# Three small moves in a hybrid encoder block: a wider product of channel factors, key reads on another queue, and additions on another engine

## The chip, the cores and the metric

The kernel runs on one core of a Trainium2 chip. A core has a matrix engine (PE), three engines for elementwise work (Vector, here DVE; Scalar, here ACT; GpSimd, here POOL) and a sync engine (SP), each with an instruction stream of its own that it works through in order, and 16 DMA engines that move data between the core's on-chip memory (SBUF) and the chip's main memory. Matrix products land in PSUM, eight banks of 512 float32 columns. DMAs are issued by SP, ACT or POOL, each with a queue. The metric is the time of the whole program on the device in microseconds.

## The reference

One layer of an encoder block, applied with the same weights to a batch of 512 tokens and one of 256 (768 rows in all), model width 2048, everything in float32:

```
h = rmsnorm(x, ln_mix_g); z = h @ w_in                 # 2048 -> 1024 fourier | 1024 q | 256 k | 256 v
of = einsum('bsgc,gcd->bsgd', Re(fft2(zf)), w_f)       # 8 groups of 128 channels, over (positions, channels)
q, k = apply_rope(q), apply_rope(k)
oa = window_attention(q, k, v, sink)                   # 16 q heads, 4 kv heads, +-128 positions
x = x + concat(rmsnorm(of), rmsnorm(oa)) @ w_out
h = rmsnorm(x, ln_mlp_g); u = relu(h @ w_up)
x = x + (u * u) @ w_down                               # 8192 wide
y = rmsnorm(x, ln_final_g)
```

## The kernel before, in words

Matrix products are done as three products of rounded halves: each operand is split into a high part (rounded for the fast matrix path, ACT) and a low remainder (DVE subtracts), and high x high, high x low and low x high are added up in PSUM. The helper `split` (L66) does both halves. Large products (the Fourier columns of `w_in`, `w_up`, `w_down`) are taken by a seven-product scheme on 2 x 2 blocks.

The program runs in stages: the values and the Fourier columns of `w_in` (to about 174 us), then twenty pieces of `w_in` for keys and queries (to 378 us), the attention together with the Fourier half of `w_out` (to 589 us), the attention half of `w_out` (to 731 us), then `w_up` and `w_down`. PE's order is that in which the code is written. On the other engines a scheduler orders the work in the pieces' stage; from the last piece on their order too is written out, by events with due times.

In the stage of pieces, PE works through the pieces (`pz`, L802, 48 matmuls each), and other work is hung on half pieces by `after(piece, fn)`:

- The Fourier groups. `load_group(g)` (L543) reads the group's map `wf` and its columns `zf` by SP. `fold(g)` (L559) forms the channel factors: the cosine and sine tables of the channels (`cc`) times the group's `w_fourier`, a product `pc` in plain float32 (L566), whose split is `cw`; it also folds the positions into sums and differences `s`. One piece later `stage1` multiplies these with `cw` (`pa`), and half a piece and a piece later the rest of `stage1` and `stage2` follow (`pe`, `pz2`). Group g's `fold` is hung on piece g + 0.5, so that of the next group comes right behind the first part of `stage1` of this one. `pc`, `pa`, `pe` and `pz2` share four PSUM banks.
- The rotation of keys and queries. `cross` (L682) multiplies by the sines on POOL (`zy`), `turned` and `parts` finish on DVE and ACT, and ACT's queue writes high and low parts of the keys (`kh`, `kl`) and the queries to main memory. `load_k(i)` (L717) reads the keys back, twice for each part, into the two halves of the partitions of `kdh` and `kdl`, four reads in all; they are hung on pieces 14.5 to 17.5.

In the attention, units of one block and one group of heads follow each other; PE forms the scores `s` (L848), DVE takes row maxima (L863), ACT the exponentials, POOL scales by the row sums (L893), PE transposes (L905) and multiplies by the values (L924). Finished row tiles of 128 tokens are read back by `load_oa` (L956): `parts_of` splits them for the product with `w_out`; `squares` squares both halves on ACT (L972) and adds them, and `reduce` (L975) sums over the head dimension on DVE into `sr`. There are six row tiles; for five the squares stand in `oar`, for the last in `cx`.

Of the kernel before, what the change touches and what calls it, by code (L numbers as in the profile page):

```python
# [11 lines left out]
F32 = mybir.dt.float32  # L12
F32R = mybir.dt.float32r
BF16 = mybir.dt.bfloat16
AF = mybir.ActivationFunctionType
ALU = mybir.AluOpType
# [4 lines left out]
P = 128  # L21
# [10 lines left out]
NKV = 4  # L32
# [8 lines left out]
def hybrid_encoder(ctx: ExitStack, tc: tile.TileContext, a: dict):  # L41
    nc = tc.nc
    ctx.enter_context(tc.manual_schedule(engines={mybir.EngineType.PE}))

    def f32(ap):
        return ap.bitcast(F32)
# [19 lines left out]
    def split(hi, lo, src, scale=None):  # L66

        if scale is None:
            nc.scalar.activation(hi, src, AF.Copy)
            nc.vector.tensor_tensor(out=lo, in0=src, in1=f32(hi), op=ALU.subtract)  # L70
        else:
            nc.scalar.activation(hi, src, AF.Copy, scale=scale)
            nc.vector.scalar_tensor_tensor(
                out=lo, in0=src, scalar=scale, in1=f32(hi), op0=ALU.mult, op1=ALU.subtract
            )
# [41 lines left out]
    kr_d = [dpool.tile([2 * P, T], F32, tag=f"k{c}", name=f"k{c}") for c in "hl"]  # L117
# [35 lines left out]
    raws = {}  # L153
# [44 lines left out]
    with ExitStack() as ph:  # L198
        hp = ph.enter_context(tc.tile_pool(name="hp", bufs=1, reuse_waits="tile"))
        pp = ph.enter_context(tc.tile_pool(name="pp1", bufs=4, space=PSUM))  # L200
# [338 lines left out]
        fp = fctx.enter_context(tc.tile_pool(name="fp", bufs=1, reuse_waits="tile"))  # L539
        cc = fp.tile([P, 2, P], F32, tag="cc", name="cc")  # L540
        ssf = fp.tile([P, T], F32, tag="ssf", name="ssf")
        fst = {}
        def load_group(g):  # L543
            wf = fp.tile([P, P], F32, tag="wf", name="wf", bufs=2)
            nc.sync.dma_start(wf[:], a["w_fourier"][g])
            z = fp.tile([P, T], F32, tag="zf", name="zf", bufs=2)
            nc.sync.dma_start(z[:], zf_d[g][:])
            fst[g] = (z, wf)

        nc.sync.dma_start(cc[:], a["c_chan"])  # L550
        load_group(0)
        tabh = fp.tile([P, 4, 256], F32R, tag="tabh", name="tabh")
        tabl = fp.tile([P, 4, 256], F32R, tag="tabl", name="tabl")
# [5 lines left out]
        def fold(g):  # L559

            z, wf = fst.pop(g)
            nc.vector.tensor_tensor(out=z[:], in0=z[:], in1=rb[:], op=ALU.mult)
            pc = pp.tile([P, 512], F32, tag="f", bufs=4, name="pc")
            cw = fp.tile([P, 2, 2, P], F32R, tag="cw", name="cw", bufs=2)
            for i in range(2):
                nc.tensor.matmul(pc[:, i * P : (i + 1) * P], cc[:, i, :], wf[:], start=True, stop=True)  # L566
            split(cw[:, 0], cw[:, 1], pc[:, :256].rearrange("p (s d) -> p s d", s=2))
            e = fp.tile([P, 320], F32, tag="fe", name="fe")
            o = fp.tile([P, 256], F32, tag="fo", name="fo")
            s = fp.tile([P, 6, P], F32, tag="fs", name="fs")  # L570
            tt = lambda out, x, y, op: nc.vector.tensor_tensor(out=out, in0=x, in1=y, op=op)
            add, sub = ALU.add, ALU.subtract
            tt(e[:, 1:256], z[:, 1:256], z[:, 511:256:-1], add)
            nc.scalar.copy(e[:, 0:257:256], z[:, 0:257:256])
            tt(o[:, 1:256], z[:, 1:256], z[:, 511:256:-1], sub)
            tt(s[:, 0, :], e[:, 0:128], e[:, 256:128:-1], add)
            tt(s[:, 1, :], e[:, 0:128], e[:, 256:128:-1], sub)
            nc.scalar.copy(s[:, 2, 0:1], e[:, 128:129])
            tt(s[:, 2, 1:128], o[:, 1:128], o[:, 255:128:-1], sub)
            tt(s[:, 3, 0:127], o[:, 1:128], o[:, 255:128:-1], add)  # L580
            nc.scalar.copy(s[:, 3, 127:128], o[:, 128:129])
            nc.scalar.copy(s[:, 4, 0:1], z[:, 512:513])
            tt(s[:, 4, 1:128], z[:, 513:640], z[:, 767:640:-1], add)
            nc.scalar.copy(s[:, 5, 0:1], z[:, 640:641])
            tt(s[:, 5, 1:128], z[:, 513:640], z[:, 767:640:-1], sub)
            sh = fp.tile([P, 6, P], F32R, tag="sh", name="sh")
            sl = fp.tile([P, 6, P], F32R, tag="sl", name="sl")
            split(sh[:], sl[:], s[:])
            ah = fp.tile([P, 6, P], F32R, tag="ah", name="ah")
            al = fp.tile([P, 6, P], F32R, tag="al", name="al")  # L590
            fst[g] = (sh, sl, cw, ah, al)
# [63 lines left out]
        kt = {}  # L655
# [60 lines left out]

        def load_k(i):  # L717
            h = slice(i % 2 * HD, (i % 2 + 1) * HD)
            nc.sync.dma_start(f32(kt["kdh" if i < 2 else "kdl"][h]), kr_d[i // 2][:].rearrange("(d h) t -> d h t", h=NKV))

        units = [(b, g) for b in range(NM) for g in range(NKV)]
        state = {}
# [14 lines left out]
        for g in range(FG):  # L737
            p0 = (0.5, 1.5, 2.5, 3.5, 4.5, 5.5, 6.5, 7.5)[g]
            if g > 0:
                after(p0 - 1, lambda g=g: load_group(g))  # L740
            after(p0, lambda g=g: fold(g))
            for b in range(3):
                after(p0 + 1 + (b == 2) * 0.5, lambda g=g, b=b: stage1(g, b))
            after(p0 + 2, lambda g=g: stage2(g))
# [10 lines left out]
        for i in range(4):  # L755
            after(14.5 + i, lambda i=i: load_k(i))
# [31 lines left out]
        for piece in range(n_in):  # L788
# [7 lines left out]
            for c in range(2):  # L796
                cs = slice(c * P, (c + 1) * P)
                for i in range(4):
                    first, stop = j == 0 and i == 0, j == 3 and i == 3
                    for w, o, n in ((wh, 0, 0), (wh, 1, 1), (wl, 0, 2)):  # L800
                        for s in range(2):
                            nc.tensor.matmul(  # L802
                                ps[c][s][:, :HALF], w[:, i, cs], whole[j // 2][s][o][:, 4 * (j % 2) + i, :],
                                start=first and n == 0, stop=stop and n == 2,
# [24 lines left out]
    op = out_ctx.enter_context(tc.tile_pool(name="op", bufs=1, reuse_waits="tile"))  # L829
# [3 lines left out]
    mask, sink, kdh, kdl = (kt[c] for c in ("mask", "sink", "kdh", "kdl"))  # L833
# [116 lines left out]
    def oa_tiles(m):  # L950

        oa[m] = [
            op.tile([P, 8, P], F32R, tag=f"of{c}{m - 1}", name=f"oa{c}{m}") for c in "hl"
        ] + [op.tile([P, P], F32, tag=f"sr{m}", name="sr")]

    def load_oa(m, when=lambda dt, fn: fn(), spare=None):  # L956

        oa_tiles(m)
        oh, ol, sr = oa[m]
        if spare is None:  # L960
            raws = [op.tile([P, 4, P], F32, tag="oar", name="oar", bufs=2)[:] for _ in range(2)]
        else:
            raws = spare
        for i, raw in enumerate(raws):
            nc.sync.dma_start(raw, oa_d[m][i * 512 : (i + 1) * 512, :].rearrange("(k p) t -> p k t", p=P))

        def parts_of(i):
            split(oh[:, 4 * i : 4 * i + 4, :], ol[:, 4 * i : 4 * i + 4, :], raws[i])

        def squares():  # L970
            for raw in raws:
                nc.scalar.activation(raw, raw, AF.Square)  # L972
            nc.gpsimd.tensor_tensor(out=raws[1], in0=raws[1], in1=raws[0], op=ALU.add)

        def reduce():  # L975
            nc.vector.tensor_reduce(out=sr[:], in_=raws[1].rearrange("p k t -> p t k"), op=ALU.add, axis=AX.X)

        when(t_oa0, lambda: parts_of(0))
        when(t_oa1, lambda: parts_of(1))
        when(max(t_sq, t_oa0, t_oa1), squares)  # L980
        when(max(t_red, t_sq, t_oa0, t_oa1), reduce)
# [22 lines left out]
    for u in range(len(units)):  # L1004
        t = pace * u + t_first
# [423 lines left out]
    pp = ctx.enter_context(tc.tile_pool(name="pp5", bufs=4, space=PSUM, reuse_waits="tile"))  # L1429
# [382 lines left out]
```

## Time and profile before

| | |
|---|---|
| median of 3 runs | 2591.28 us (2590.07 to 2592.25) |
| the profiled execution | 2589.57 us |
| its span, first to last instruction | 2587.7 us |
| granted PE clock | 0.999 of full speed |
| PE busy | 2576.2 us (100% of the span) |
| DVE, ACT, POOL busy | 1812.2, 1124.0, 257.8 us |
| moved by DMA | 489.55 MB |

A row of a group reads: line, engine, operation, output <- inputs, shapes, count, then busy us, mean ns of one, and idle us before it with what ended it. A row of a timeline or of the chain in order of time starts with its start and its duration in us; the brackets hold the idle time before it and what ended that. A row of a waiting list reads: us in total, times, the longest. A row of a windows table has the stretch, its length, the busy us of PE, PEld (weight loads), DVE, ACT and POOL with their instructions, the granted clock, the DMA engines' busy share and GB/s.

### The profile page before, as it was taken

To read this page: it belongs to the slowest core of one execution; us is meant where nothing else is said; L and a number is where in the kernel's file an instruction comes from. 1 tells how busy PE (TensorE), PEld (TensorE's weight loads), DVE (VectorE), ACT (ScalarE), POOL (GpSimd) and SP (SyncE) were. 2 spreads that over 40 slices of the span, in tenths; PEclk is the share of its full clock that TensorE was granted. 3 is DMA by queue.
4 is the path that set the end of the run, shared out by engine and by line. 5 is a ranking of instruction groups with operands and counts; after the bars stand their busy time and mean duration, and the time that the engine had idled before them with its cause. 6 is when DMAs were issued, how large, how long until landed. Compare 5 with 4: busy or idle time off the path is not lost.

```text
span 2587.7 us, 34958 instructions
## 1 busy us (share of the span) xinstructions
PE 2576.2 (100%) x13580; PEld 2358.4 (91%) x13580; DVE 1812.2 (70%) x2216; ACT 1124.0 (43%) x1574; POOL 257.8 (10%) x359
## 2 busy tenths in 40 slices
PE   9999999999999999999999999999999999999998
PEld 9999998888899999999999999988888888888887
DVE  7966568777555656555877877667776765777687
ACT  6545437674333333333444544433333333333335
POOL 1001332233201011000000000110000000000000
PEclk9999999999999999999999999999999999999999
DMA  7963385345664445456666666675543662555364
GB/s 252 311 226 113 127 240 181 117 135 193 223 193 157 163 160 186 161 190 238 213 214 232 229 215 208 248 301 178 182 156 111 220 232 82 179 179 164 96 209 155
DMA packets 268999, 489.55 MB, mean 189 GB/s; under 512 B 19568, under 2 KB 164000, under 8 KB 267424
## 3 DMA queue, kind: packets, MB, share of 16 engines
q1 hardware_dynamic: 197328, 321.26, 39.3%
q10 hardware_dynamic: 58688, 115.18, 11.7%
q0 software_dynamic: 12816, 50.87, 5.8%
q8 instruction: 107, 1.75, 0.3%
q14 instruction: 60, 0.49, 0.1%
HBM read 360.35 MB, written 126.88 MB: 188 GB/s over the span
## 4 chain that ended last, share of the span: by engine, by line
PE 98%; DVE 1%; DMA 1%; issue 0%; ACT 0%; DVEq 0%; SPq 0%; POOLq 0%; POOL 0%; ACTq 0%
PE pu L1193 36%; PE pd L1628 35%; PE pm L1046 9%; PE pz L802 6%; PE p L268 5%; PE pv L391 1%; PE o L924 1%; PE s L848 1%; PE t L905 1%; PE pe L630 0%; PE pa L609 0%; PE ptx L137 0%; DMA raw<-in_w_in 0%; PE pt L137 0%; DMA qs<-ql 0%; PE pz L630 0%
## 5 line engine op out<-in xcount | busy, mean ns | idle before, releaser
L1193 PE MATMUL pu<-xf,wh 128*128 128x384 f32 x3072 | 780.1, 334 | 0.0
L1193 PEld LDWEIGHTS pu<-xf,wh 128*128 128x128 f32 x3072 | 554.0, 188 | 1.5 <-ACT o L1211 1.1
L1628 PE MATMUL pd<-wl,sh 128*128 128x512 f32 x1332 | 517.8, 389 | 0.0
L1628 PE MATMUL pd<-wh,sh 128*128 128x512 f32 x1332 | 517.8, 389 | 0.0
L1628 PE MATMUL pd<-wh,sl 128*128 128x512 f32 x1332 | 517.6, 389 | 0.0
L1193 PE MATMUL pu<-xf,wl 128*128 128x384 f32 x1536 | 513.2, 334 | 0.0
L1605 ACT ACTIVATE wh<-rd 128x1024 fp32r<-128x1024 f32 x200 | 202.4, 1054 | 522.2 <-PE pd L1628 421.8
L1615 DVE TENSOR_TENSOR wl<-rd,wh 128x1024 fp32r<-128x1024 f32 x200 | 236.1, 1221 | 226.3 <-ACT wh L1605 225.5
L1173 ACT ACTIVATE wh<-ur 128x1024 fp32r<-128x1024 f32 x160 | 170.0, 1063 | 382.7 <-PE pu L1193 216.8
L1628 PEld LDWEIGHTS pd<-wh,sh 128*128 128x128 f32 x1332 | 250.0, 188 | 51.9
L1628 PEld LDWEIGHTS pd<-wl,sh 128*128 128x128 f32 x1332 | 250.0, 188 | 51.9
L1628 PEld LDWEIGHTS pd<-wh,sl 128*128 128x128 f32 x1332 | 249.9, 188 | 51.8 <-DVE sl L1616 0.3
L1193 PEld LDWEIGHTS pu<-xf,wl 128*128 128x128 f32 x1536 | 288.3, 188 | 0.0
L1179 DVE TENSOR_TENSOR wl<-ur,wh 128x1024 fp32r<-128x1024 f32 x160 | 195.4, 1221 | 75.4 <-ACT wh L1173 75.4
L1214 DVE TENSOR_TENSOR o<-pu,o 128x768 f32<-128x768 f32 x160 | 152.8, 955 | 123.3 <-PE pu L1193 115.1
L1598 DVE TENSOR_TENSOR rd<-rd 128x1024 f32<-128x1024 f32 x112 | 131.7, 1217 | 0.0
L1193 PE MATMUL pu<-xs,wh 128*128 128x384 f32 x512 | 129.8, 334 | 0.0
L1173 ACT ACTIVATE wh<-sx 128x1024 fp32r<-128x1024 f32 x64 | 67.9, 1062 | 130.4 <-PE pu L1193 101.9
L268 PE MATMUL p<-xs,wh 128*128 128x384 f32 x448 | 113.8, 334 | 0.0
L1616 DVE TENSOR_TENSOR sl<-sr,sh 128x768 fp32r<-128x768 f32 x111 | 105.5, 950 | 0.0
L1179 DVE TENSOR_TENSOR wl<-sx,wh 128x1024 fp32r<-128x1024 f32 x64 | 78.1, 1222 | 24.1 <-ACT wh L1173 23.9
L1193 PEld LDWEIGHTS pu<-xs,wh 128*128 128x128 f32 x512 | 92.4, 188 | 0.0
(279 smaller groups left out, 3921.9 us busy)
## 6 DMA issues: line engine op xcount, KB each, us to landing
rd<-in_w_down SPq DMA_DIRECT2D x176, 512.0 KB, 5.2
ur<-in_w_up SPq DMA_DIRECT2D x128, 512.0 KB, 3.9
sr<-sd SPq DMA_DIRECT2D x95, 384.0 KB, 5.4
pd<-o ACTq DMA_DIRECT2D x60, 384.0 KB, 2.3
o<-pd POOLq DMA_DIRECT2D x60, 384.0 KB, 6.0
sd<-sm ACTq DMA_DIRECT2D x60, 384.0 KB, 2.8
raw<-in_w_in SPq DMA_DIRECT2D x38, 512.0 KB, 6.0
raw<-in_w_out SPq DMA_DIRECT2D x32, 512.0 KB, 4.5
```

The lines of the kernel that those rows point to most:

```text
L268: nc.tensor.matmul(ps7[bank, g, r][:, :HALF], l[:, i, r * P : (r + 1) * P], x[:, o, 4 * e + i, :], start=(opens and e == 0 and i == 0 and ...
L802: nc.tensor.matmul(ps[c][s][:, :HALF], w[:, i, cs], whole[j // 2][s][o][:, 4 * (j % 2) + i, :], start=first and n == 0, stop=stop and n == 2,)
L1046: nc.tensor.matmul(ps, l(k), w[:, k % 2, :], start=(k == 0 and n == 0), stop=(k == 7 and n == 2))
L1173: nc.scalar.activation(wh[:], raw[:], AF.Copy)
L1179: nc.vector.tensor_tensor(out=wl[:], in0=raw[:], in1=f32(wh[:]), op=ALU.subtract)
L1193: nc.tensor.matmul(ps[:, t, :HALF], w[:, i, t * P : (t + 1) * P], xb[:, o, i, :], start=(s == first_of[bank] and i == 0 and n == 0), stop= ...
L1214: nc.vector.tensor_tensor(out=o, in0=src, in1=o, op=ALU.add)
L1598: add = lambda x, y, op: nc.vector.tensor_tensor(out=x[:], in0=x[:], in1=y[:], op=op)
L1605: nc.scalar.activation(wh[:], t[:], AF.Copy)
L1615: nc.vector.tensor_tensor(out=wl[:], in0=t[:], in1=f32(wh[:]), op=ALU.subtract)
L1616: nc.vector.tensor_tensor(out=sl[:], in0=sr[:], in1=f32(sh[:]), op=ALU.subtract)
L1628: nc.tensor.matmul(o, l[:, q, ts], w[:, ns], start=(j == j0 and (q, t) == (0, 0)), stop=(j == j1 and (q, t) == (1, 2)),)
```

## The change

Three edits. The channel factors of two Fourier groups are formed at once: the maps of groups g and g + 1 (g even) are read by one DMA and stand side by side, one product per table has 256 columns in place of 128, one split of 512 columns makes both groups' `cw`, and the odd group's `fold` takes its half from there. The four reads of the rotated keys are issued on GpSimd's queue in place of SP's. The sum of the two squared halves of an attention row tile is formed by Vector in place of GpSimd.

```diff
-        fst = {}
+        fst, cws = {}, {}
         def load_group(g):
-            wf = fp.tile([P, P], F32, tag="wf", name="wf", bufs=2)
-            nc.sync.dma_start(wf[:], a["w_fourier"][g])
+            if g % 2 == 0:
+                wf = fp.tile([P, 2, P], F32, tag="wf", name="wf")
+                nc.sync.dma_start(wf[:], a["w_fourier"][g : g + 2].rearrange("g c d -> c g d"))
+            else:
+                wf = None
...
             nc.vector.tensor_tensor(out=z[:], in0=z[:], in1=rb[:], op=ALU.mult)
-            pc = pp.tile([P, 512], F32, tag="f", bufs=4, name="pc")
-            cw = fp.tile([P, 2, 2, P], F32R, tag="cw", name="cw", bufs=2)
-            for i in range(2):
-                nc.tensor.matmul(pc[:, i * P : (i + 1) * P], cc[:, i, :], wf[:], start=True, stop=True)
-            split(cw[:, 0], cw[:, 1], pc[:, :256].rearrange("p (s d) -> p s d", s=2))
+            if wf is not None:
+                pc = pp.tile([P, 512], F32, tag="f", bufs=4, name="pc")
+                cws["now"] = fp.tile([P, 2, 2, 2, P], F32R, tag="cw", name="cw", bufs=2)
+                for i in range(2):
+                    nc.tensor.matmul(pc[:, i * 256 : (i + 1) * 256], cc[:, i, :], wf[:].rearrange("c g d -> c (g d)"), start=True, stop=True)
+                both = [cws["now"][:, o].rearrange("p g s d -> p (g s) d") for o in range(2)]
+                split(*[x.rearrange("p (g s) d -> p s g d", g=2) for x in both], pc[:].rearrange("p (s g d) -> p s g d", s=2, g=2))
+            cw = cws["now"][:, :, g % 2]
...
         def load_k(i):
             h = slice(i % 2 * HD, (i % 2 + 1) * HD)
-            nc.sync.dma_start(f32(kt["kdh" if i < 2 else "kdl"][h]), kr_d[i // 2][:].rearrange("(d h) t -> d h t", h=NKV))
+            nc.gpsimd.dma_start(f32(kt["kdh" if i < 2 else "kdl"][h]), kr_d[i // 2][:].rearrange("(d h) t -> d h t", h=NKV))
...
         def squares():
             for raw in raws:
                 nc.scalar.activation(raw, raw, AF.Square)
-            nc.gpsimd.tensor_tensor(out=raws[1], in0=raws[1], in1=raws[0], op=ALU.add)
+            nc.vector.tensor_tensor(out=raws[1], in0=raws[1], in1=raws[0], op=ALU.add)
```

Line numbers behind the edit are shifted by 3 to 6: L566 becomes L570, L719 becomes L725, L973 becomes L979.

## The prediction

> **What bounds the kernel now.** I read the page's first table and its chain of waits, then the list of waits on PE, then, place by place, the chain in order of time, the timelines and the windows around the three edits.
>
> ```profile
> span 2587.7 us, 34958 instructions
> PE 2576.2 (100%) x13580; PEld 2358.4 (91%) x13580; DVE 1812.2 (70%) x2216; ACT 1124.0 (43%) x1574; POOL 257.8 (10%) x359
> PE 98%; DVE 1%; DMA 1%; issue 0%; ACT 0%; DVEq 0%; SPq 0%; POOLq 0%; POOL 0%; ACTq 0%
> ...
> PE pv L391 <- ACT wh L69: 1.1, 1, 1.1
> PE pw L474 <- DVE mhalf L56: 1.0, 1, 1.0
> PE s L848 <- DMA qs<-ql: 0.4, 1, 0.4
> PE pt L137 <- DVE xr L452: 0.2, 1, 0.2
> PE pt L137 <- DMA xt<-in_x_prompt: 0.2, 1, 0.2
> ```
>
> The chain that ended last is PE for 98% of the span, and the whole list of what PE waited for adds up to 2.9 us, of which only the 0.4 us for `qs` lies after the first 60 us. So this is a PE program nearly from end to end: an edit shortens the run only by what it takes out of PE's own stream, and lengthens it only by making PE wait where it doesn't now. A microsecond won on DVE, POOL or SP is worth nothing by itself. The profiled execution took 2589.57 us, 1.87 us more than its span of 2587.7, and is 1.71 us under the median of 2591.28; I work out differences and apply them to the median.
>
> **The change, first edit: two groups' channel factors at once.** This one alone touches PE's stream. In the chain of waits in order of time, the product `pc` of a group shows as one piece, and the summary line of the stretch from 174 to 302 us gives its share:
>
> ```profile
> by line: PE pz L802 71.8%; PE pe L630 8.9%; PE pa L609 8.7%; PE pz L630 4.5%; PE pc L566 3.1%; PE pa L598 1.8%; PE pa L599 0.8%; PE ps_r L648 0.5%
> ...
> 186.44 0.44 PE pc L566 x4
> 222.01 0.50 PE pc L566 x4
> 231.56 1.43 PE pe L630 x12
> ```
>
> 3.1% of 128 us is 4.0 us for eight groups, 0.50 us each. A group has two matmuls in the program and four records (x4), so each matmul of plain float32 runs as two records, 0.125 us per record. In PE's order the second group of each pair loses its product:
>
> ```order
> L599 MATMUL pa<-cw,sl 128x128
> L609 MATMUL pa<-cw,sh 128x256 x2
> L609 MATMUL pa<-cw,sl 128x256
> L609 MATMUL pa<-cw,sh 128x128 x2
> L609 MATMUL pa<-cw,sl 128x128
> L566 MATMUL pc<-wf,cc 128x128 x2
> L802 MATMUL pz<-xs_291,wh 128x384
> ```
>
> That is the place before, in the second group; now:
>
> ```order
> L605 MATMUL pa<-cw,sl 128x128
> L615 MATMUL pa<-cw,sh 128x256 x2
> L615 MATMUL pa<-cw,sl 128x256
> L615 MATMUL pa<-cw,sh 128x128 x2
> L615 MATMUL pa<-cw,sl 128x128
> L808 MATMUL pz<-xs_291,wh 128x384
> ```
>
> The row of `pc` is gone, and the first group's row reads 128x256 x2 in place of 128x128 x2: half the records with twice the columns. No float32 product in the trace has more than 128 columns, so the price of a wide record is bounded. End A: it costs what a 256-column record of the rounded type costs, 1.43 / 12 = 0.119 us. Then a pair takes 4 x 0.119 = 0.48 us instead of 2 x 0.50 = 1.00, and four pairs save 4 x 0.52 = 2.1 us. End B: time goes with columns, a record takes 0.25 us, and nothing is saved. Two sets of rows from PE's timeline pull either way:
>
> ```profile
> 233.67 0.22 PE L599 MATMUL pa<-cw,sl 128*128 128x128 f32 x1
> 233.73 0.34 PE L598 MATMUL pa<-cw,sh 128*128 128x256 f32 x1
> ...
> 594.79 0.50 PE L1367 MATMUL pr<-ones,sr 128*128 128x1 f32 x4
> 595.15 0.49 PE L1046 MATMUL pm<-wh,oah 128*128 128x512 f32 x1
> ```
>
> A 128-column record of the rounded type is followed after 0.06 us, half of a `pc` record's step: plain float32 looks bound by columns, at half the rate (end B). But four float32 records of a single column also take 0.36 us, 0.09 each: there is a floor that has nothing to do with columns, and halving the records saves it (end A). The row of the same kind, `pc` itself, stands only a little above that floor. I take a third of the way from B to A, a gain of 0.7 us, and keep 0 to 2.1 for the range. A loss is excluded here: the columns are the same in all, and the records half.
>
> The Trainium skill (FP8 and Floating Point Precision, TensorE Precision Notes) says that true FP32 takes four passes through the array, two halves against two halves. The trace agrees as far as it goes, with two records of twice the usual step. By that rule the wide product costs its full columns and the term would be end B, zero.
>
> The split of `cw` becomes one 512-column operation in the first group and none in the second. Its price: the same split of a 512-column bank in the attention,
>
> ```profile
> L909 DVE TENSOR_TENSOR tl<-t,th 128x512 fp32r<-128x512 f32 x56 | 37.8, 677 | 2.5 <-ACT th L908 2.5
> ...
> 226.30 0.41 DVE L70 TENSOR_TENSOR cw<-pc,cw 128x256 fp32r<-128x256 f32 x1
> ...
> 232.27 0.28 DVE L70 TENSOR_TENSOR al<-pa,ah 1x128 fp32r<-1x128 f32 x1
> ...
> 233.43 0.28 PE L630 MATMUL pz<-tabh,al 128*128 128x256 f32 x1
> ```
>
> 0.68 against 0.41 us, so DVE's row in the first group of a pair runs 0.27 us later and in the second 0.41 earlier. Behind it the tightest consumer is the last `al` row, done at 232.55 and read by PE at 233.43: 0.88 us of cover, so I cost the delay at nothing. If ACT's longer half adds as much again (0.5 us in all) the cover still holds; were it gone entirely, four groups could lose at most 0.5 us each, 2 us. The four `wf` loads dropped from SP's queue were issued without PE waiting, and the one that is left per pair is needed as late as before: nothing.
>
> **Second edit: the key reads move to POOL's queue.** They leave SP, where each stood in line behind a weight load, and come to stand on POOL:
>
> ```order
> L687 TENSOR_TENSOR zy<-zs,sinr 128x256 x28
> L893 TENSOR_SCALAR p<-p,rs 128x256 x8
> L893 TENSOR_SCALAR p<-p,rs 128x384 x12
> L687 TENSOR_TENSOR zy<-zs,sinr 128x256 x2
> L893 TENSOR_SCALAR p<-p,rs 128x384 x8
> ```
>
> That is POOL around the rotation before (`zy` is the crossed product with the sines), and now:
>
> ```order
> L693 TENSOR_TENSOR zy<-zs,sinr 128x256 x12
> L725 DMA kdh<-kh 64x3072 x2
> L725 DMA kdl<-kl 64x3072 x2
> L693 TENSOR_TENSOR zy<-zs,sinr 128x256 x16
> L899 TENSOR_SCALAR p<-p,rs 128x256 x8
> ```
>
> All four stand after the twelfth `zy` and hold the other sixteen behind them. The timelines say whether that is a wait:
>
> ```profile
> 320.57 6.65 POOL L687 TENSOR_TENSOR zy<-zs,sinr 128x256 f32<-128x256 f32 x4 [1.99 <-DVE zs L696]
> 344.50 0.73 POOL L687 TENSOR_TENSOR zy<-zs,sinr 128x256 f32<-128x256 f32 x1 [17.27 <-ACT zs L815]
> ...
> 324.48 0.37 ACTq L704 DMA_DIRECT2D kl<-zs  x1
> ...
> DMA to landing us min/median/max: 2.1/2.5/4.6
> ...
> 339.67 0.51 SPq L719 DMA_DIRECT2D kdl<-kl  x1
> 344.04 0.47 SPq L719 DMA_DIRECT2D kdl<-kl  x1
> ...
> L848 PE MATMUL s<-kdl,qs x96: 274/281/421, 378.0 to 573.6; 128*128 128x256 f32 x64, 128*128 128x384 f32 x32
> ```
>
> The last write of the keys goes out at 324.48 and lands some 2.5, at most 4.6, us later (the row for those writes), by 329.1; POOL ends its twelfth `zy` at 327.2 and has nothing to do until 344.5. So the four reads go out some 12 us sooner than the last ones on SP, inside a hole of 17.27 us, and PE first reads the keys at 378.0. The other side is traffic:
>
> ```profile
> 323.00:345.00 22.00, 22.00 (x127) 21.64 (x126) 12.86 (x16) 7.82 (x8) 4.72 (x4) 1.00 0.94 278
> ...
> 333.12 0.40 SPq L79 DMA_DIRECT2D raw<-in_w_in  x1
> ...
> 337.22 2.01 DVE L70 TENSOR_TENSOR wl<-raw,wh 128x1024 fp32r<-128x1024 f32 x1 [2.57 <-ACT wh L69]
> 341.58 2.01 DVE L70 TENSOR_TENSOR wl<-raw,wh 128x1024 fp32r<-128x1024 f32 x1 [2.36 <-ACT wh L69]
> ...
> 302.85 75.20 PE pz L802 x431
> ```
>
> From 323 to 345 us the DMA engines are 94% busy, and the same 3.1 MB (four times 64 x 3072 floats) now come earlier in that stretch and compete with the weight load of 333.12. The pieces of `w_in` whose low halves are done at 339.2 and 343.6 are the last but two and the last but one. The last nine pieces run as one block on PE from 302.85 for 75.20 us, 8.36 each, so PE opens these two at 353.0 and 361.3: covers of 13.8 and 17.7 us. A load later by even 10 us costs nothing.
>
> **Third edit: DVE adds the squares.** Six additions of 512 columns leave POOL (1.29 us each) and come to DVE. In DVE's order at the third row tile, before:
>
> ```order
> L863 ISA p,mx<-s,mask,sink 128x256
> L863 ISA mx 128x1
> L868 TENSOR_SCALAR nm<-mx 128x1
> L976 TENSOR_REDUCE sr<-oar 128x128
> L863 ISA p,mx<-s,mask,sink 128x256
> ```
>
> and now, the same place (`oar` the squares, `p,mx` the row maxima that free a score bank):
>
> ```order
> L869 ISA p,mx<-s,mask,sink 128x256
> L869 ISA mx 128x1
> L874 TENSOR_SCALAR nm<-mx 128x1
> L979 TENSOR_TENSOR oar<-oar 128x512
> L982 TENSOR_REDUCE sr<-oar 128x128
> L869 ISA p,mx<-s,mask,sink 128x256
> ```
>
> The new row waits for ACT's squares, with row maxima, `tl` splits and the normalising factors queued behind it. DVE's waiting list and the timelines of that tile:
>
> ```profile
> DVE p L863 <- PE s L848: 7.7, 13, 0.9
> DVE sr L976 <- POOL oar L973: 2.7, 3, 1.6
> ...
> 565.50 1.14 ACT L972 ACTIVATE oar<-oar 128x512 f32<-128x512 f32 x2
> ...
> 566.31 0.15 DVE L868 TENSOR_SCALAR nm<-mx 128x1 f32<-128x1 f32 x1
> 568.11 1.09 DVE L976 TENSOR_REDUCE sr<-oar 128x128 f32<-128x512 f32 x1 [1.64 <-POOL oar L973]
> ...
> L70 DVE TENSOR_TENSOR oal<-oar,oah 128x512 fp32r<-128x512 f32 x10 | 7.4, 738 | 1.9 <-ACT oah L69 1.9
> ```
>
> ACT ends the squares at 566.64, 0.2 us after DVE gets there; the addition costs what the like-sized `oal` row costs, 0.74 us, and the reduction starts about 567.4 instead of 568.11. Here DVE wins 0.7 us; where the old reduction didn't wait it loses 0.74. DVE already waits for PE's scores 13 times, so it runs ahead of PE, and nothing of either sign reaches PE: zero.
>
> The sum is 0.7 + 0 + 0, so 2591.28 - 0.7 = 2590.6 us.
>
> A rule that speaks for a little more relief: while POOL added,
>
> ```profile
> 575.63 1.28 POOL L973 TENSOR_TENSOR oar<-oar 128x512 f32<-128x512 f32 x1 [0.69 <-ACT oar L972]
> ...
> L870 DVE TENSOR_TENSOR es<-sink,mx x24: 151/153/1164, 387.3 to 575.8; 128x4 f32<-128x4 f32 x24
> ```
>
> a DVE row of 0.15 us took 1.16. The Trainium skill (SBUF — State Buffer, SBUF: two separate sides) has DVE operations with two SBUF inputs and POOL's share an exclusive port pair. The trace agrees. As DVE is off PE's path the sum is the same with and without it.
>
> **The rivals.** *Nothing gained* (end B): two records of 256 columns take what four of 128 did, 2591.3 us; it lies within the same band, and for it speaks the 0.06 us row. *Slower: POOL's key reads land too late.* Four reads from 327.2 have 50.8 us until 378.0, 12.7 us each if POOL's queue served them one after the other; on SP they landed within 10.9. Were they to take 15 us each, PE would stand still for 9 us at its first scores, 2600 us; it decides from 12.7 us each. Against it: they need not be served singly. The skill's same section warns that descriptors written by POOL starve while DVE holds the port, which speaks for it; no run here shows it for these reads. *Slower by DVE's new wait*, 1 us in each of six tiles, would need DVE to lose its whole lead over PE: 2597 us. *Faster beyond the product*: all of `pc` and the `qs` wait together are 4.4 us, which sets a floor of 2586.9; only PE work that I haven't seen could go beyond.
>
> **How the numbers follow.** A measurement of this kernel can tell about 0.2%, 5.2 us, from no change. My forecast with its bounds has 0.60, nothing gained 0.27, the two slower rivals 0.05 and 0.03, faster than the floor allows 0.05. The range takes in both ends of the product (0 to 2.1 us saved), 2 us for a lost cover in the Fourier groups, and 1.2 us of spread between runs to the low side: 2588.0 to 2593.3. Chances: faster 0.05, same 0.87, slower 0.08.
>
> **What would show it.** Right: 16 `pc` records instead of 32, together 2 to 4 us of the chain; PE's list of waits as it is now; POOL's four reads issued near 327 us and landed long before 378; no wait of `sr` for POOL, and the new addition near 0.74 us. Wrong: PE waiting for `al`, `kd` or DVE's row maxima by more than 2 us in all, or a wide `pc` record above 0.25 us.

## The result and the profile after

The changed kernel takes 2602.1 us (median of 6 runs, 2601.05 to 2604.04) against 2591.44 us (2590.07 to 2592.25, 6 runs) for the kernel before: a ratio of 1.0042, 95% interval 1.0031 to 1.0053, or 10.7 us longer. The forecast was 2590.6 us, with 2588.0 to 2593.3 as its range.

The first lines of the page after:

```profile
span 2602.3 us, 34913 instructions
PE 2579.2 (99%) x13564; PEld 2361.6 (91%) x13564; DVE 1812.7 (70%) x2218; ACT 1123.3 (43%) x1570; POOL 256.4 (10%) x357
```

PE's list of waits after (total us, times, longest):

```profile
PE pz L808 <- ACT zs L821: 9.7, 1, 9.7
PE pt L137 <- DMA xt<-in_x_prompt: 1.7, 1, 1.7
...
PE pc L570 <- ACT of L638: 0.3, 1, 0.3
```

There is one new wait of size. PE stands still 9.7 us, once, in the stage of pieces, until ACT has copied (`zs`, L821) the finished sums `pz` of one pair of columns out of PSUM, so that the next pair can have the banks. The 1.7 us for `xt` lie in the first 15 us, where none of the three edits reaches; other runs below show 0.2 to 1.3 us there. Windows after, around the wait (length, busy us of PE, PEld, DVE, ACT and POOL, granted clock, DMA share, GB/s):

```profile
346.00:350.00 4.00, 0.42 (x3) 0.10 (x1) 0.00 (x0) 0.00 (x0) 0.00 (x0) 0.82 1.01 301
350.00:356.00 6.00, 0.00 (x0) 0.00 (x0) 2.73 (x3) 4.70 (x5) 0.00 (x0) 0.50 0.61 213
356.00:362.00 6.00, 5.87 (x18) 5.78 (x19) 2.31 (x2) 2.95 (x5) 2.33 (x2) 0.50 0.56 175
362.00:364.00 2.00, 2.00 (x12) 2.00 (x12) 1.67 (x1) 0.25 (x1) 2.00 (x1) 0.95 0.00 0
```

PE is idle until 356.1, and the clock, 1.00 before, is then at 0.50 until about 362.2: about 6.1 us at half speed cost another 3.0. The 14.6 us between the two spans (2602.3 and 2587.7) are thus 9.7 of standing still, 3.0 of slow clock, 1.5 more of `xt`, and 0.4 of small things. The profiled execution is the slowest of the six; no trace of the others was kept.

What held ACT's copies up is read from ACT's timeline. Before:

```profile
333.29 0.63 ACT L709 ACTIVATE zh<-zs 128x512 fp32r<-128x512 f32 x1 [4.01 <-DMA qh<-zh]
...
343.88 0.86 ACT L815 COPY zs<-pz 128x384 f32<-128x384 f32 x2 [2.33 <-DMA ql<-zs]
```

and after:

```profile
332.33 0.48 ACTq L710 DMA_DIRECT2D qh<-zh  x1
332.90 0.42 ACTq L710 DMA_DIRECT2D ql<-zs  x1
350.07 0.63 ACT L715 ACTIVATE zh<-zs 128x512 fp32r<-128x512 f32 x1 [18.45 <-DMA qh<-zh]
350.73 0.37 ACTq L710 DMA_DIRECT2D qh<-zh  x1
351.46 0.37 ACTq L710 DMA_DIRECT2D ql<-zs  x1
351.93 3.83 ACT L69 ACTIVATE wh<-raw 128x1024 fp32r<-128x1024 f32 x2 [1.22 <-DMA raw<-in_w_in]
355.54 0.91 ACT L821 COPY zs<-pz 128x384 f32<-128x384 f32 x2
```

ACT writes a pair's rotated queries in three parts, each a high half `qh` and a low half `ql`. The third high half `zh` needs the buffer of the first, so it waits until the first `qh` write has landed: 4.01 us before, 18.45 after. Behind it in ACT's order stand the third pair of writes, the splits of two weight pieces, and then the copies that PE waits for. The row at 343.88 before shows a second tie: the copy writes into the pair's `zs` buffer, which the last `ql` write reads, and it had been waiting 2.33 us for that write already. PE's timeline before says how much cover there was:

```profile
344.42 1.19 PE L802 MATMUL pz<-xf,wh 128*128 128x384 f32 x4
```

The first product into the freed banks starts at 344.42, while the two copies run (343.88 to 344.74). The cover was nil, and the delay reached PE in full: the copies start 11.66 us later after the change (355.54), PE's own stream was 2.0 us behind by then (it would have begun at 346.42), and the rest, 9.7 us, is the wait.

The writes landed late because of what moved beside them. POOL's rows for the reads, after, with their time to landing:

```profile
L725 POOL DMA_DIRECT2D kdh<-kh x2: 513/564/616, 329.5 to 330.1; - x2
L725 POOL DMA_DIRECT2D kdl<-kl x2: 509/513/517, 331.0 to 331.5; - x2
...
DMA to landing us min/median/max: 6.4/12.0/17.8
```

All four reads, 3.1 MB, are posted within 2.5 us and landed by 349.3. The DMA view by queue (packets, MB, summed time of the packets as a share of the 16 engines, which can pass 100%; q0 is GpSimd's queue, q1 SP's, q10 ACT's), after, from 332 to 336 and from 340 to 344 us:

```profile
q0 software_dynamic: 93, 0.95, 109.2%
...
q0 software_dynamic: 62, 0.58, 61.7%
q1 hardware_dynamic: 70, 0.22, 25.1%
q10 hardware_dynamic: 66, 0.07, 9.3%
```

and before, from 330 to 334 us:

```profile
q10 hardware_dynamic: 1285, 1.24, 90.2%
q1 hardware_dynamic: 19, 0.06, 12.8%
```

Before, ACT's queue had the engines nearly to itself for these 4 us and moved 1285 packets of about 1 KB. After, GpSimd's reads alone moved from 332 to 336, in packets of 0.95 MB / 93 = 10 KB, although writes had been posted from 330.99 on; from 340 to 344 the three queues moved nearly equal numbers of packets, 62, 70 and 66, so that the queue with 1-KB packets got 0.07 MB where it had got 1.24.

The Trainium skill (DMA: Bandwidth & Descriptors, Queues, rings and completion order) says that each DMA engine takes the queues in turn, a packet at a time. The trace agrees from about 338 us on, in that the counts are nearly equal; the page's packet holds several descriptors, typically 9 to 17, and no run here shows whether the profile's packets are that unit. Why GpSimd's queue had the engines alone before 338 us isn't shown either. One more transfer was slowed, SP's read of another pair's sums (`zs`, 0.79 MB, posted at 330.59), which took 19.2 us in place of 5.1; no wait of PE is put down to it.

### The profile page after: what moved, and what is told of

It reads as the page before. It is cut to its first block, busy times and chain, and to the rows that moved or that the text cites. A ratio compares the mean times of both kernels' runs of the same rounds, so it can differ in the third digit from the quotient of the medians.

```text
span 2602.3 us, 34913 instructions
## 1 busy us (share of the span) xinstructions
PE 2579.2 (99%) x13564; PEld 2361.6 (91%) x13564; DVE 1812.7 (70%) x2218; ACT 1123.3 (43%) x1570; POOL 256.4 (10%) x357
## 4 chain that ended last, share of the span: by engine, by line
PE 92%; DVE 3%; issue 2%; DMA 1%; POOL 1%; ACT 1%; SPq 0%; ACTq 0%; POOLq 0%; DVEq 0%
PE pu L1199 36%; PE pd L1634 35%; PE pm L1052 10%; PE p L268 4%; PE pz L808 2%; PE o L930 1%; PE s L854 1%; PE t L911 1%; POOL zy L693 1%; PE pv L391 1%; DMA raw<-in_w_in 1%; DVE wl L70 0%; PE ptx L137 0%; PE pe L636 0%; DMA raw<-in_w_out 0%
```

## The experiments

Eleven kernels were run. Where a ratio is given, it is to the kernel before on the same chip.

**e1: the key reads back on SP's queue** (the other two edits stay):

```diff
-            nc.gpsimd.dma_start(f32(kt["kdh" if i < 2 else "kdl"][h]), ...)
+            nc.sync.dma_start(f32(kt["kdh" if i < 2 else "kdl"][h]), ...)
```

> The changed kernel with the four key reads back on SP's queue, so the wide product and Vector's add alone are left. Theory A (the reads on GpSimd's queue cost all of the loss): PE's wait of 9.7 us for the pz evacuation is gone, ACT's wait of 18.45 us for the qh write is back to about 4 us, and the time is 2590.6 us, 0.7 under the kernel before (2588.7 to 2591.4 by the bounds of the prediction for the wide product). Rival B (the wide product or Vector's add shifted something that makes the stall): the wait stays and the time is 2600 us or more.

Measured: 2591.13 us (2589.87 to 2595.92), ratio 1.0003 (0.9994 to 1.0012). PE's wait at this place:

```profile
PE pz L808 <- ACT zs L821: 0.2, 1, 0.2
```

The whole loss is gone with the reads. The interval, about -1.6 to +3.1 us, can't tell a gain of 0.7 us from none. That 0.2 us of waiting is left shows once more that this place has no cover.

**e2: the reads alone on GpSimd's queue**, the kernel before with only the `load_k` line of the diff.

> The kernel before with the four key reads on GpSimd's queue and nothing else. Theory A: PE waits 9 to 10 us for a pz evacuation, the granted clock is down for some microseconds behind it, and the time is 2601 to 2604 us. Rival B: 2591 to 2592 us and no such wait.

Measured: 2602.92 us, ratio 1.0046 (1.0033 to 1.006).

```profile
PE pz L802 <- ACT zs L815: 9.5, 1, 9.5
```

The second edit by itself makes the wait and the loss; rival B is out.

**e3: a buffer of its own for the third high half**: for `s == 2`, `hi` comes from another pool with one buffer.

```diff
-            hi = kt["kp"].tile([P, 2, 256], F32R, tag="zy" if pair == len(cols) - 1 else "qs", name="zh", bufs=2)
+            own = s == 2 and pair < len(cols) - 1
+            hi = (zo["p"] if own else kt["kp"]).tile([P, 2, 256], F32R, tag="zh" if own else "zy" if pair == len(cols) - 1 else "qs", name="zh", bufs=1 if own else 2)
```

> The changed kernel, where the third high half of each rotated pair has a buffer of its own, so that ACT need not wait for the first qh write to land. Theory A1 (the jam holds up both the qh writes and the w_in load that SP issues at 334.8, which lands 17.5 us later): ACT no longer stands for the qh write, but the weight split ahead of the evacuations still waits for that load until about 352, so PE's wait stays 8 to 9.7 us and the time 2600 to 2602 us. Rival A2 (the buffer of the high half is the only link): PE's wait falls under 2 us and the time is 2591 to 2593 us.

Measured: 2600.99 us, ratio 1.0039 (1.0025 to 1.0052), PE's wait 9.2 us. ACT's timeline:

```profile
333.70 0.63 ACT L716 ACTIVATE zh<-zs 128x512 fp32r<-128x512 f32 x1 [1.96 <-DVE zs L702]
334.37 0.37 ACTq L711 DMA_DIRECT2D qh<-zh  x1
335.52 9.93 ACTq L711 DMA_DIRECT2D ql<-zs  x1
...
352.91 2.00 ACT L69 ACTIVATE wh<-raw 128x1024 fp32r<-128x1024 f32 x1 [5.35 <-DMA raw<-in_w_in]
355.31 0.86 ACT L822 COPY zs<-pz 128x384 f32<-128x384 f32 x2 [0.40 <-DMA ql<-zs]
```

ACT no longer waits for `qh` and is 16 us earlier at the third half, and it brings nothing: the split waits for the weight load, as expected, and the copy for the last `ql` write, which I had not named. The buffer is one of three ties to the same jam. With it gone the other two end within 0.4 us of each other (the split at 354.91, the `ql` write at 355.31), so either would by itself have held PE nearly as long.

**e4: shorter packets**, each read cut in two by time.

```diff
-            nc.gpsimd.dma_start(f32(kt["kdh" if i < 2 else "kdl"][h]), ...)
+            for t in (slice(0, HALF), slice(HALF, T)):
+                nc.gpsimd.dma_start(f32(kt["kdh" if i < 2 else "kdl"][h, :, t]), src[:, :, t])
```

> The changed kernel, where each of the four key reads on GpSimd's queue is cut into two by time, so that its packets are 1.5 KB (384 columns) in place of 12 KB; bytes, queue and place in the order are the same. Theory A3 (a DMA engine takes a packet of each queue in turn, so that a write in 1-KB packets waits 12 KB for each of its own): the first qh write lands within 8 us of its issue in place of 19, the w_in load within 12 in place of 17.5, PE's wait is under 2.5 us and the time 2590 to 2594 us. Rival A4 (reads on GpSimd's queue go ahead of the other queues whatever their packets, or the 3.1 MB alone decide): the qh write lands 15 to 20 us after its issue, the wait stays 8 us or more and the time 2600 us or more.

Measured: 2601.6 us, ratio 1.004 (1.0026 to 1.0054), PE's wait 8.9 us. The DMA view from 340 to 344 us, and ACT's timeline:

```profile
q0 software_dynamic: 212, 0.74, 66.8%
q1 hardware_dynamic: 212, 0.22, 19.1%
q10 hardware_dynamic: 211, 0.20, 16.6%
```

```profile
338.02 0.63 ACT L715 ACTIVATE zh<-zs 128x512 fp32r<-128x512 f32 x1 [7.48 <-DMA qh<-zh]
...
349.07 2.00 ACT L69 ACTIVATE wh<-raw 128x1024 fp32r<-128x1024 f32 x1 [7.20 <-DMA raw<-in_w_in]
354.22 0.86 ACT L823 COPY zs<-pz 128x384 f32<-128x384 f32 x2 [3.16 <-DMA ql<-zs]
```

Each theory has half of it: the landing of the first write is as A3 said, PE's wait and the time are as A4 said. The trace doesn't show the 1.5 KB that were planned: 0.74 MB in 212 packets are 3.5 KB each on average, in place of 9 (0.58 MB in 62). The nearly equal counts are there again, 212, 212 and 211 packets. ACT's queue moves three times the bytes (0.20 MB against 0.07), and the first `qh` write lands in 8.0 us in place of 19. But the time stays, because the later transfers land no earlier: the weight load after 17.1 us, the last `ql` write at about 354. Shorter packets changed who was served first; the 3.1 MB ahead of the last write stayed the same, which is the likely reason that it landed no earlier. Packets of 1.5 KB stay untested.

**e5: half of the reads**, only `kdh` on GpSimd's queue.

```diff
-            nc.gpsimd.dma_start(f32(kt["kdh" if i < 2 else "kdl"][h]), ...)
+            (nc.gpsimd if i < 2 else nc.sync).dma_start(f32(kt["kdh" if i < 2 else "kdl"][h]), ...)
```

> The changed kernel, where only the two kdh reads go on GpSimd's queue and the two kdl reads stay on SP's. Theory B (what decides is when the last write of the pair before, ql, lands: ACT's evacuation of the next pz goes into the buffer that this write reads, and the write must get through beside whatever is in flight): with 1.57 MB less in flight the first qh write lands about 340, the last ql about 346, and PE's wait falls from 9.7 us to between 0 and 3 us; time 2591 to 2595 us. Rival (PE's wait goes with the bytes that GpSimd's queue carries): half of it, 4 to 5 us of wait, 2596 to 2598 us.

Measured: 2598.3 us, ratio 1.0029 (1.0019 to 1.0039), PE's wait 5.1 us; the copy that ended it:

```profile
351.19 0.86 ACT L821 COPY zs<-pz 128x384 f32<-128x384 f32 x2 [2.27 <-DMA ql<-zs]
```

My number (0 to 3 us) was too low, the rival's about right: half the bytes, half the wait. The mechanism is the same, the copy waits for the last `ql`; I had put its landing at 346.

**e6: the same burst later**; DVE first writes a column of `kdh` and of `kdl` out of the pair-3 tile, so that the reads can't go before the copy.

```diff
-            after(14.5 + i, lambda i=i: load_k(i))
+            if i % 2 == 0:
+                after(15, lambda c="hl"[i // 2]: nc.vector.tensor_copy(kt["kd" + c][:, 0, 0:1], zt[3][:, 1, T - 1 : T]))
+            after(15, lambda i=i: load_k(i))
```

> The changed kernel with all four reads still on GpSimd's queue, back to back and with their 12-KB packets, but later: Vector first writes one column of kdh and of kdl from the pair-3 tile (overwritten by the reads), so that they can't go out before the pz evacuation. Theory B (the place is the fault, not the queue): the reads go out near 349 us, behind the writes, the evacuation is on time, PE doesn't wait, the keys land by 368 and before 378; 2590 to 2593 us. Rival (reads in one burst on GpSimd's queue stop the others wherever they stand): PE waits 5 us or more for the next evacuation or its first keys, 2596 us or more.

Measured: 2598.2 us, ratio 1.0026 (1.0016 to 1.0036). PE's list of waits:

```profile
PE s L856 <- DMA qs<-ql: 5.8, 1, 5.8
```

The wait for the copies is gone, as expected, and another has come: the burst, now posted from 350.7 to 352.8, sits on the writes of the next pair (352.9 to 357.0), which take 16.6 us to land, the last pair's are late in turn, and PE stands still 5.8 us for its first query rows. I had expected no wait; the rival is right: the burst costs wherever such writes stand beside it.

**e9: the late burst on SP's queue**, as e6 but with `nc.sync` for the reads.

> The late reads of the run e6 (four key reads held until the pz evacuation, back to back, 12-KB packets), but on SP's queue. Theory C (a burst of 12-KB packets that stands beside the writes slows them on either kind of queue, since an engine serves the queues a packet at a time): the writes of pair 3, issued some microseconds behind the reads, take 12 us or more to land, as they took 16.6 on GpSimd's queue, PE waits 4 us or more for the first query rows, 2596 us or more. Rival D (GpSimd's queue is special): beside SP's burst these writes land within 7 us of their issue, and PE's wait for the query rows is under 2 us unless SP's own order makes it.

Measured: 2597.23 us, ratio 1.0024 (1.0013 to 1.0035), PE's wait for the query rows 3.9 us. The first three `qh` writes of pair 3:

```profile
DMA to landing us min/median/max: 6.4/6.4/7.8
```

This looks like the rival, but it wasn't the same burst, by SP's timeline:

```profile
349.54 1.15 SPq L725 DMA_DIRECT2D kdh<-kh  x2
361.48 8.18 SPq L725 DMA_DIRECT2D kdl<-kl  x2
```

SP issued two reads and stood until 361.5 before the third; its list of waits puts 10.7 us there down to a `qh` write that had not landed. So only half of the 3.1 MB was in flight beside these writes, and theory C isn't tested by them. PE's 3.9 us came later: the query rows were read from 378.55 on, once a `qh` write had landed that was posted at 369.58 and took 8.8 us, beside the last key read on SP's queue (posted at 369.2). The next run puts half of the reads on GpSimd's queue at the same place.

**e10: half of the late burst on GpSimd's queue**: the gate of e6, the two `kdh` reads by `nc.gpsimd`, the two `kdl` reads by `nc.sync` two pieces later.

> Only the two kdh reads of the late reads on GpSimd's queue (near 350 us, as in the run e6), the two kdl reads on SP's queue behind pair 3's rotation; it stands against the run e9, which had two kdh reads in flight on SP's queue at the same place, where the first two qh writes of pair 3 took 7.8 and 6.4 us to land. Theory C (either kind of queue slows the writes alike for the same bytes in flight): the first writes of pair 3 land within 6 to 9 us. Rival D (GpSimd's queue is worse byte for byte): they take 10 us or more. The time of the whole isn't the question; the later kdl reads may cost some microseconds at 378.

Measured, in a single execution (2596.18 us): the first `qh` write of pair 3 took 7.8 us to land, and its first two `ql` writes:

```profile
DMA to landing us min/median/max: 7.5/7.6/7.7
```

Beside two reads on SP's queue the writes took 4.9 to 7.8 us (`ql` 4.9 to 6.1), beside two on GpSimd's 7.5 to 7.8, beside four on GpSimd's 16.6. The first `qh` write, posted at 353.63 and 353.35, took 7.8 us in both runs; the later ones stand at other distances from their reads, so a difference of some 2 us between the queues isn't excluded. The DMA views show the same picture too: from 354 to 358 us, with ACT's first writes posted, only the reads moved, 86 packets of SP's queue in e9 and 91 of GpSimd's here. PE's wait in this run, 5.0 us at its first scores, ended with the query rows, not with the keys: the rows were read from 379.07 on, once a `qh` write had landed that was posted at 368.24 and took 10.7 us, beside the two late `kdl` reads on SP's queue (posted from 367.5 on). So writes stood late beside reads on SP's queue as well, as theory C has it. What differs is mainly how much gets in flight: POOL had nothing else to do and posted four reads in 2.5 us, while SP, before the change, posted them one by one from 324.1 to 344.0 us, with weight loads between them that wait for their buffers.

**e11: one read in flight at a time** on GpSimd's queue, from the same early place: between two reads POOL copies a column of the one that has landed into the place of the next.

```diff
+            if i:
+                was = kt["kdh" if i < 3 else "kdl"][(i - 1) % 2 * HD : ((i - 1) % 2 + 1) * HD]
+                nc.gpsimd.tensor_copy(kt["kdh" if i < 2 else "kdl"][h, 0, 0:1], f32(was[:, 0, 0:1]))
             nc.gpsimd.dma_start(f32(kt["kdh" if i < 2 else "kdl"][h]), ...)
```

> The changed kernel with all four key reads on GpSimd's queue from 329.5 us on, but one in flight at a time: between two reads GpSimd copies one column of the read that has landed into the place of the next, which holds the next read back (the column is overwritten). Theory B (the backlog of four reads is what holds up the writes): each read lands within 7 us, the last near 352; the first qh write lands within 8 us of its issue, the last ql by 346, and PE's wait is under 2 us; 2590 to 2594 us. Rival (any 12-KB packets of GpSimd's queue beside the writes cost the same): the writes crawl as long as the reads last, PE's wait stays 7 us or more, 2599 us or more.

Measured: 2594.02 us (2593.02 to 2595.61), ratio 1.0013 (1.0003 to 1.0022). The wait, and the windows over it:

```profile
PE pz L811 <- ACT zs L824: 2.1, 1, 2.1
```

```profile
346.00:350.00 4.00, 2.60 (x9) 2.42 (x10) 2.33 (x2) 4.00 (x6) 2.28 (x1) 0.78 0.93 204
350.00:354.00 4.00, 4.00 (x20) 4.00 (x20) 2.28 (x2) 0.40 (x2) 2.32 (x4) 0.79 0.65 186
```

Same queue, same packets, nearly the same start (328.0 us): with one read in flight in place of four, 7.6 of the 9.7 us of waiting are gone. But holding the reads back also puts fewer of them ahead of the copies at 346.83, by POOL's timeline:

```profile
335.09 0.52 POOL L728 DMA_DIRECT2D kdh<-kh  x1 [0.29 <-POOL kdh L727]
344.98 0.51 POOL L728 DMA_DIRECT2D kdl<-kl  x1 [0.39 <-POOL kdl L727]
352.13 0.57 POOL L728 DMA_DIRECT2D kdl<-kl  x1 [0.29 <-POOL kdl L727]
```

The run e5 had the same two `kdh` reads ahead of its copies, both in flight at once, and its third read went out at 343.13, and PE waited 5.1 us there. By this comparison about 4.6 of the 7.6 us go with the smaller amount and 3.0 with the spacing. The first `qh` write lands in 7.2 us, as expected; the last read goes out at 352.13 and lands at about 360, not near 352, and the wait and the time end just above what was expected. This kernel is still slower than the one before.

**e7 and e8: the price of the wide product** by itself: each product of the channel factors issued nine times, in the kernel before and in the one with the reads on SP.

```diff
-                nc.tensor.matmul(pc[:, i * P : (i + 1) * P], cc[:, i, :], wf[:], start=True, stop=True)
+                for _ in range(9): nc.tensor.matmul(pc[:, i * P : (i + 1) * P], cc[:, i, :], wf[:], start=True, stop=True)
```

> The kernel before with each of the sixteen products of 128 columns issued nine times in place of once, the result the same: 256 records more on PE. With the prediction's 0.125 us each it is 32 us longer, 2623 us. It stands against the next run, which does the same with the wide product.

> The kernel with the wide product and Vector's add and the key reads on SP's queue, each of the eight products of 256 columns issued nine times: 128 records more on PE. By the prediction's end A (0.119 us for a wide record) it is 15 us longer than with one, 2606 us, and 17 us under the narrow one; by end B (0.25 us) 32 us longer and level with the narrow one; by the value that was taken (a third of the way) 26 us longer and 5.6 under it.

Measured: 2620.16 us narrow (2618.7 to 2621.2) and 2618.71 us wide (2617.27 to 2621.15). The chain in order of time (start, duration), one row of the narrow kernel

```profile
199.92 4.07 PE pc L566 x36
```

and one of the wide:

```profile
216.25 7.82 PE pc L570 x36
```

A narrow record takes 4.07 / 36 = 0.113 us, a wide one 7.82 / 36 = 0.217. The times agree within their noise: 28.98 us more than before for 256 records are 0.113 each, and 27.58 us more than with the reads on SP (e1, another chip) for 128 records are 0.215. A pair of groups pays 8 x 0.113 = 0.904 us narrow and 4 x 0.217 = 0.869 wide. Four pairs save 0.14 us: end B, all but exactly.

## Why the prediction was wrong

**The first edit: the mechanism was right, the size was off.** The term was 0.7 us, taken a third of the way between 0 and 2.1; it measures 0.14 in the two runs above, and 0.3 by the rows of the changed kernel itself, where a pair takes 0.92 us in place of twice 0.50:

```profile
236.71 0.92 PE pc L570 x4
```

PE's time for plain float32 went with the columns here, 0.113 us for 128 and 0.217 for 256. I had weighed the floor of single-column records too highly: at 128 columns the record is already past it. By the Trainium skill's four passes (FP8 and Floating Point Precision, TensorE Precision Notes) the term was zero, and the traces now agree: twice the columns, 1.92 times the duration. The delay of `al` had its cover in the changed kernel, as said, but barely: in the runs e3, e4 and e5 PE waited for it once, for 0.3 to 0.4 us. PE's list shows 0.3 us for a bank at `pc`, once, and in the kernel with the reads alone it is there too.

**The second edit: the step that failed is the one called traffic.** It says that the reads "compete with the weight load of 333.12", that PE opens the two weight pieces 13.8 and 17.7 us after their halves are done, and concludes: "A load later by even 10 us costs nothing." The load was posted 1.7 us later and took 17.5 us to land in place of 6.3, so it came 12.9 us later, and PE's list indeed has no wait for weights. But the reads competed with more than that load. ACT's writes of the pair's queries were in flight too, four of the six from 330.99 to 333.3; they were not in the list. Their cover was not 13.8 us but nil, and the trace before showed it: ACT's copy at 343.88 had waited 2.33 us for a `ql` write, with PE at the freed banks by 344.42. Nor was the load off ACT's path: its split stands ahead of the same copies in ACT's order, so the cover that counted was the copies', not PE's reading of the weights. In the changed kernel it landed at 352.3, while ACT was at the split before, and held nothing up; in e3 ACT waited 5.35 us for it.

**The rest of the second edit held.** The reads went out at 329.5 into POOL's hole (forecast: 327) and landed by 349.3, 28 us ahead of the 378.0 at which PE had read the keys before and 43 ahead of its first scores now (392.4). The rival "POOL's key reads land too late" gives 2600 us, near the result, by another mechanism; it was not what happened.

**The third edit: right.** DVE's rows for the addition, after:

```profile
L979 DVE TENSOR_TENSOR oar<-oar x5: 681/693/693, 479.8 to 595.7; 128x512 f32<-128x512 f32 x5
```

0.69 us each (forecast 0.74), `sr` no longer waits for POOL, and DVE waits 0.7 us once for ACT's squares; PE's list has nothing of it. The kernel with the first and third edits alone stands level with the one before. None of the versions beats it by an amount that could be told.

**The price of a stall.** The rivals were priced by the wait alone. In these runs a stall also brought the slow clock behind it, so the 9.7 us cost some 12.7 in the profiled execution.

## What to carry to other kernels

When a transfer moves to an idle engine's queue, it can lose the waits that kept it apart from other transfers: list every DMA in flight in the new stretch, of all queues and in both directions, and find for each who waits for its landing, first of all an in-order engine with a PSUM evacuation behind that wait. The cover of a late write is read where its buffer is next written: a wait for a write that is in the trace already, on the engine that frees PE's banks, means that the cover is nil. And a product in plain float32 gained nothing that the time of this kernel shows from going to half as many instructions of 256 columns in place of 128.

## What the runs showed of the hardware

- **A stall of 2.1 us brought a whole interval of slow clock.** From the granted clock in the windows, the time at 0.50 comes out as 13.6 us for the 9.7-us stall after, 10.2 for the 9.5-us one of the reads alone, 3.4 for the 5.1 of half the reads, and 3.4 (0.22 x 4 + 0.21 x 4 us, divided by 0.5) even for the 2.1 us of one read at a time: multiples of 3.4 us, partly during the stall and partly behind it. The Trainium skill (TensorE: Matmul & The Clock Gate, Part 1) has half rate after an idle window of some 3.4 us; the lengths agree, and here 2.1 us of idle time were enough. A wait of 0.9 us in the same run, for query rows, brought none.
- **Packets of unlike size share by number, not by bytes**: 62, 70 and 66 packets of 9, 3 and 1 KB on average in the same 4 us; and a queue with a backlog had the engines nearly alone at first: from 330 to 336 us after, GpSimd's queue moved 119 packets and ACT's 8, and from 354 to 358 in e9 SP's moved 86 and ACT's none.
- **Issuing one DMA took an engine 9.93 us.** In the run with a third buffer, ACT's sixth write took that long to issue, at a time when its five earlier writes had not landed, against 0.37 us as a rule and 2.11 at most for such writes in the other runs. Why isn't shown.
